# A two-layer trunk on one core: queues reordered, five joints between stages laid out anew, and attention begun inside the last expert tiles

## The chip, the cores and the metric

The kernel runs on one core of a Trainium2 chip. The metric is the device time of one execution in microseconds, as the median of several runs.

## The reference

Input is x, 512 rows of 1024 float32. Two layers follow, each a mixer and an expert block, each behind a root-mean-square norm with a gain, each added to x:

```python
for layer in range(DEPTH):                       # DEPTH = 2
    h = rms_norm(x, norm_mix)
    x = x + (even_mix(h, ...) if layer % 2 == 0 else fox_mix(h, ...))
    h = rms_norm(x, ffn_norm[layer])
    x = x + peer_ffn(h, wq, keys, u, v)
```

`even_mix` projects h to 2576 columns, runs a gated depthwise convolution of width 31 with a layer norm on one half and a chunked gated linear attention on the other, and projects the 1024 results back. `fox_mix` projects h to q, k, v (16 heads of 64) and a forget gate, normalises q and k per head, adds the running sums of the log forget gate to the logits, and takes a causal softmax. `peer_ffn` picks, for each row and each of 8 heads, 16 of 16384 experts by two sets of 128 keys, and adds `gate * gelu(h . u[e]) * v[e]` over these 128 experts.

## The kernel before

**Precision.** Every matmul with a weight is done in three passes: a float32 operand is split into a high part, rounded to float32r by ScalarE, and a low part, the difference, taken by VectorE (or POOL). `split` (line 49) does that, `weight` (54) loads a 128x1024 weight tile into one of four `raw` buffers, and splits it into one of three pairs `whi`, `wlo`; `mm3` (75) issues high x high, high x low and low x high.

**Blocks.** The 512 rows are four blocks of 128. `rms_h` (87) and `rms_body` (95) normalise: per block a square with its sum on ScalarE (104), the factor on VectorE and POOL (105, 106), the scaled rows on VectorE (107) into one of two buffers; then `flip` (109) transposes the block by eight 128x128 matmuls into two PSUM banks (114), from which ScalarE copies the high part (116) and VectorE takes the low part (117) of the transposed `hT`. `hT` has a single buffer pair for all stages.

**Stages.** `build` (1060) runs `mix_even` (228), `peer(0)`, `mix_odd` (542), `peer(1)` (719). The code is unrolled; a tracing framework orders each engine's instructions by a simulated timeline, with program order as priority, and sets the semaphores. `tc.issue_after(i)` ties the instructions traced in it behind instruction `i` on the engine of `i`.

**The mixers** end in `out_proj` (194): two halves of 512 columns, each four weight tiles (`proj_nat`, 145; `nat_parts`, 153) over four accumulators of the six PSUM banks tagged `a`; in the second half the last three weight tiles are swept block by block in the order 1, 2, 3, 0, and each block is added to x. In `mix_odd` the value projection's first half is begun on two leading weight tiles, block by block as the blocks are transposed. Attention's logits, softmax, transposes and values go in 64 units of 128 queries of one head (`unit`, 682), four inside each of 14 q or k projections, the last twelve behind them.

**The expert block** treats block 0 by gathering each row's experts (POOL's indirect loads, lines 861 and 872) and blocks 1 to 3 densely: a first half of 128 tiles (`u_step`, 842: one weight tile, 24 matmuls of 384 columns, a Gelu, a store to `aside`, of which the last 24 stay on chip), during which the gate values are built by small matmuls (`gate4`, 891) and stored to `G`; and a second half of 128 tiles (`prepare`, 962, `v_sweep`, 1022: 18 matmuls of 512 columns into six accumulators). `fetch` (950) loads gates, eight tiles at a time (`gc`), and kept activations, two tiles at a time (`at`). The last three tiles of the second half are swept block by block (1052). `kept` (725) is a copy of blocks 1 to 3 of x in memory, from which x is read back later.

**Queues.** All plain loads and stores are issued by SP, in order; POOL issues the gathers. A load of a weight waits for its `raw` buffer. Line 544 asks for the function table that has logarithm and exponential, tied behind `last_gelu`, which is set by `u_step` (853) and, later, by the gathers' Gelu `g_w` (867).

## Time and profile before

| | us |
|---|---|
| median of 3 runs | 3146.25 (3145.14 to 3149.17) |
| the profiled execution | 3148.14 |
| its span, first to last instruction | 3146.3 |
| mean granted TensorE clock | 0.990 |

The profiled execution is a little longer than its span, by what lies ahead of the first and behind the last instruction. The stages in the span: even mixer to about 271 us, first experts to 1545 (their second half from 1012), attention to 1867, second experts to the end (their second half from 2609). In what follows PE is TensorE's matmuls, PEld its weight loads, DVE VectorE, ACT ScalarE, POOL GpSimd, SP the queue of plain loads. A line of the timeline gives the start, the length, the engine, the source line and what is written from what; in brackets stands the engine's idle time before it and what ended that.

### The profile page before, as it was taken

How to read it: one execution, taken by the hardware profiler on the slowest of the kernel's cores; microseconds unless marked ns; L12 is line 12 of the kernel's file. 1: busy time of each engine (PE TensorE's matmuls, PEld its weight loads, DVE VectorE, ACT ScalarE, POOL GpSimd, SP SyncE). 2: the span in 40 equal slices, each digit the busy share in tenths (PEclk: the TensorE clock that was granted, in tenths of full speed). 3: DMA queues.
4: the chain of work that ended last, by engine and by line, in shares of the span. 5: the costliest groups of instructions: out<-in, count | busy, mean ns of one | idle time of the engine just before them, and what ended most of it. 6: DMA issues, size and time to landing. Idle time of an engine off the chain costs nothing.

```text
span 3146.3 us, 45733 instructions
## 1 busy us (share of the span) xinstructions
PE 3080.9 (98%) x15932; PEld 2696.8 (86%) x15932; DVE 2406.8 (76%) x4936; ACT 1437.2 (46%) x2258; POOL 1155.1 (37%) x800
## 2 busy tenths in 40 slices
PE   8999999999999999999999999999999999999999
PEld 6668999999999888877766679999999998888787
DVE  6765998888885888888535548998888867888786
ACT  4343334666664333333356633336666643333332
POOL 1220122996773332332100000227976752233330
PEclk9999999999999999999999999999999999999999
DMA  4113445999998999999421124448999997999996
GB/s 155 54 34 125 137 140 168 358 351 347 339 323 292 310 350 372 352 350 356 148 81 41 41 77 132 137 144 313 375 340 339 339 322 260 354 367 346 355 349 233
DMA packets 334202, 787.16 MB, mean 250 GB/s; under 512 B 26745, under 2 KB 181770, under 8 KB 327826
## 3 DMA queue, kind: packets, MB, share of 16 engines
q1 hardware_dynamic: 260242, 515.76, 47.0%
q0 software_dynamic: 73728, 268.47, 24.1%
q8 instruction: 125, 2.05, 0.3%
q14 instruction: 107, 0.88, 0.1%
HBM read 687.59 MB, written 96.47 MB: 249 GB/s over the span
## 4 chain that ended last, share of the span: by engine, by line
PE 90%; DVE 3%; DMA 2%; issue 1%; ACT 1%; SPq 1%; POOL 1%; DVEq 0%; ACTq 0%; POOLq 0%
PE acc L1027 33%; PE pu L79 10%; PE pu L78 10%; PE pu L77 10%; PE bank L77 5%; PE bank L79 5%; PE bank L78 5%; PE bank L911 5%; PE po L671 1%; PE pc L284 1%; PE bank L639 1%; PE bank L935 1%; DVE wlo L51 1%; SPq L960 1%; POOL gr L861 1%
## 5 line engine op out<-in xcount | busy, mean ns | idle before, releaser
L50 ACT ACTIVATE whi<-raw 128x1024 fp32r<-128x1024 f32 x604 | 636.9, 1057 | 829.5 <-PE pu L78 471.6
L51 DVE TENSOR_TENSOR wlo<-raw,whi 128x1024 fp32r<-128x1024 f32 x565 | 692.1, 1226 | 183.1 <-ACT whi L50 156.3
L77 PE MATMUL pu<-hhi,whi 128*128 128x384 f32 x2048 | 702.0, 343 | 9.6 <-ACT whi L50 8.7
L79 PE MATMUL pu<-hhi,wlo 128*128 128x384 f32 x2048 | 691.0, 338 | 2.2 <-DVE wlo L51 2.2
L78 PE MATMUL pu<-hlo,whi 128*128 128x384 f32 x2048 | 689.2, 337 | 0.0
L872 POOL DMA_INDIRECT gr<-in_vF_dram,ids x256 | 317.7, 1241 | 717.7 <-DVE x L874 658.7
L1027 PE MATMUL acc<-wlo,wh 128*128 128x512 f32 x1536 | 472.7, 389 | 0.0
L1027 PE MATMUL acc<-whi,wl 128*128 128x512 f32 x1536 | 472.5, 389 | 0.0
L1027 PE MATMUL acc<-whi,wh 128*128 128x512 f32 x1536 | 436.5, 390 | 9.3 <-ACT whi L50 9.3
L861 POOL DMA_INDIRECT gr<-in_uN_dram,ids x256 | 352.5, 1377 | 237.6 <-DVE dots L863 140.7
L50 ACT ACTIVATE wh<-gc 128x384 fp32r<-128x384 f32 x256 | 134.4, 525 | 645.7 <-PE acc L1027 638.0
L77 PEld LDWEIGHTS pu<-hhi,whi 128*128 128x128 f32 x2048 | 388.3, 190 | 12.1 <-ACT whi L50 9.3
L79 PEld LDWEIGHTS pu<-hhi,wlo 128*128 128x128 f32 x2048 | 387.3, 189 | 4.0 <-DVE wlo L51 3.9
L78 PEld LDWEIGHTS pu<-hlo,whi 128*128 128x128 f32 x2048 | 388.1, 190 | 1.9 <-DVE hlo L117 0.6
L1027 PEld LDWEIGHTS acc<-whi,wh 128*128 128x128 f32 x1536 | 287.6, 188 | 72.1 <-ACT whi L50 12.6
L1027 PEld LDWEIGHTS acc<-wlo,wh 128*128 128x128 f32 x1536 | 288.3, 188 | 60.0
L1027 PEld LDWEIGHTS acc<-whi,wl 128*128 128x128 f32 x1536 | 288.3, 188 | 59.8
L901 POOL TENSOR_SCALAR a<-cst,sT 128x128 f32<-128x128 f32 x192 | 330.6, 1722 | 13.2 <-PE bank L911 4.9
L874 DVE SCALAR_TENSOR_TENSOR x<-gr,dots,x 128x1024 f32<-128x1024 f32 x256 | 327.4, 1279 | 0.3
L863 DVE CUSTOM_DVE_ANT_0 gr<-gr,h 128x1024 f32<-128x1024 f32 x256 | 307.9, 1221 | 23.8 <-DMA gr<-in_uN_dram,ids 23.7
L51 DVE TENSOR_TENSOR wl<-gc,wh 128x384 fp32r<-128x384 f32 x256 | 142.7, 558 | 179.4 <-ACT wh L50 170.0
L51 POOL TENSOR_TENSOR wlo<-raw,whi 128x1024 fp32r<-128x1024 f32 x39 | 99.0, 2540 | 398.5 <-ACT whi L50 390.5
(248 smaller groups left out, 4242.3 us busy)
## 6 DMA issues: line engine op xcount, KB each, us to landing
raw<-in_uT_dram SPq DMA_DIRECT2D x256, 512.0 KB
raw<-in_vF_dram SPq DMA_DIRECT2D x256, 512.0 KB
G<-big SPq DMA_DIRECT2D x48, 1024.0 KB
gc<-G SPq DMA_DIRECT2D x32, 1536.0 KB
aside<-xact SPq DMA_DIRECT2D x208, 192.0 KB
at<-aside SPq DMA_DIRECT2D x104, 384.0 KB
raw<-in_w_in_dram SPq DMA_DIRECT2D x32, 512.0 KB
raw<-in_wq_dram SPq DMA_DIRECT2D x32, 512.0 KB
```

Source lines behind the costliest of these rows:

```text
L50: first = self.nc.scalar.activation(hi, raw, AF.Copy)
L51: self.last_lo = (eng or self.nc.vector).tensor_tensor(lo, raw, hi.bitcast(F32), op=ALU.subtract)
L77: mm(out, lh, rh, start=first, stop=False)
L78: mm(out, lh, rl, start=False, stop=False)
L79: return mm(out, ll, rh, start=False, stop=last)
L861: nc.gpsimd.indirect_dma_start(out=r, out_offset=None, in_=uN, in_offset=bass.IndirectOffsetOnAxis(ap=ids[:, s:s + 1], axis=0))
L863: return lambda: nc.vector.tensor_tensor_reduce(r, r, h0, 1.0, 0.0, ALU.mult, ALU.add, accum_out=dots[:, s:s + 1])
L872: nc.gpsimd.indirect_dma_start(out=r, out_offset=None, in_=vF, in_offset=bass.IndirectOffsetOnAxis(ap=ids[:, s:s + 1], axis=0))
L874: return lambda: nc.vector.scalar_tensor_tensor(self.x0, r, dots[:, s:s + 1], self.x0, op0=ALU.mult, op1=ALU.add)
L901: (nc.vector if t else nc.gpsimd).tensor_scalar(a1[:, t], self.iota, e1[:, t:t + 1], gate[:, t:t + 1], op0=ALU.is_equal, op1=ALU.mult)
L911: nc.tensor.matmul(p[:, t], a2[:, t], a1[:, t], start=True, stop=True)
L1027: nc.tensor.matmul(acc[b][c], wt[:, s], vt[:, c], start=(n == 0 and wt is wh and vt is vh), stop=(n == NE1 - 1 and wt is wl))
```

## The change

- **Norms.** `rms_h` and `rms_body` become `norm`, which hands out its steps (`scale`, `flip`, `close`) so that they can be placed one by one. The square writes into the buffer of the scaled rows; there are three or four of these in place of two and a separate square.
- **`chain`** ties each step that it runs behind the last matmul of the step before, on TensorE.
- **Start.** The gain of the first norm is loaded as one row and spread over the partitions by two matmuls with ones and two copies. The blocks of x are asked for next, then four weights (`early`), then the rest of the constants. The step tables are loaded and copied in `peer(0)`, by POOL.
- **`out_proj`** sweeps block by block in a chain, normalises blocks 1 to 3 as each is done, and stores `kept` there. In attention it also runs four units after each weight tile of the first half, and transposes blocks 1 and 2 ahead of block 0's last three sweeps and block 3 ahead of the last of them. After the even mixer the three blocks are transposed behind the sweeps, since `hT` is still in use.
- **`peer`** runs the first expert tile ahead of transposing block 0.
- **Second half of the experts.** `fetch` starts seven tiles (`SETTLE`) after its buffers are opened, its loads are tied behind the last weight's load on SP, and the split of the gates is tied behind the high part of the weight on ScalarE. The split gates have a pool of their own.
- **Into attention.** `odd_begin` runs ahead of the last tiles' sweeps: the function table, tied behind the last Gelu of both kinds, the buffers, and the first two value weights, split ahead into a pool of their own. Sweeps, additions, norms, transposes and the first value sweeps then follow in one chain. The forget gate's projection is moved ahead of the rest of the value projection.
- The convolution's diagonal matrices have three buffers in place of four.

```diff
     def weight(self, src, shape=None, eng=None, after=None, pool=None):
-        raw = self.ws.tile([P, D], F32, tag="raw", name="raw", bufs=4)
-        nc.sync.dma_start(raw, src)
+        raw = self.early.pop(0) if self.early else self.raw(src)
+        if pool:
+            hi, lo = [pool.tile([P, D], F32R, name=x) for x in ("vhi", "vlo")]
...
+    def chain(self):
+        last = []
+        def run(f, *args):
+            if last:
+                with self.tc.issue_after(last.pop().ins):
+                    last.append(f(*args))
+            else:
+                last.append(f(*args))
+            return last[0]
+        return run
...
     def nat_parts(...)
             for kp in order[lead:end]:
-                sweep(load([kp]), range(NB))
+                with self.tc.issue_after(self.last_put.ins) if pool else nullcontext():
+                    ws = load([kp])
+                sweep(ws, range(NB))
...
     def out_proj(self, w, yT, i, order=range(4), hT=None, between=None, middle=None):
...
+            def finish(b):
+                add(1, b, acc[b])
+                if b:
+                    nc.sync.dma_start(self.kept[b - 1], self.xb[b])
+                    scale(b)
+            for b in DB:
+                for f in sweeps:
+                    run(f, b)
+                finish(b)
+            for n, f in enumerate(sweeps):
+                if hT and n == 0:
+                    run(flip, 1, hT)
+                    run(flip, 2, hT)
+                if hT and n == 2:
+                    run(flip, 3, hT)
+                run(f, 0)
+            finish(0)
...
     def mix_even(self):
+        with tc.tile_pool(name="gain", bufs=1, side="right", reuse_waits="tile") as gp:
+            g = gp.tile([1, D], F32, name="g")
+            row = gp.tile([1, P], F32, name="row")
+            nc.vector.memset(row, 1.0)
+            nc.sync.dma_start(g, A["gains"][0:1])
+            for c in range(2):
+                p = self.bank()
+                nc.tensor.matmul(p, row, g[:, c * 512:(c + 1) * 512], start=True, stop=True)
+                nc.scalar.activation(self.grow[:, c * 512:(c + 1) * 512], p, AF.Copy)
+        for b in range(1, NB):
+            nc.sync.dma_start(self.xb[b], A["x"][b * P:(b + 1) * P])
+        self.early = [self.raw(A["w_in0"][i]) for i in (0, 4, 3, 7)]
...
-        with tc.issue_after(self.last_gelu.ins):
+        with tc.issue_after(self.last_gelu.ins), tc.issue_after(self.last_act.ins):
             nc.scalar.preload_act_table_set("natural_log_exp_and_others")
...
     def mix_odd_body(self, hT, sc, rest):
-            vproj(0, rest())
             fh, fl = self.small_weight(sc, A["w_fz"], 16, "wf")
...
+            vproj(0, rest())
...
-            for _ in range(8 + AHEAD + 1):
-                unit()
-            self.out_proj(A["w_out1"], self.rows(oT))
+            self.hT = self.new_hT()
+            self.out_proj(A["w_out1"], self.rows(oT), 3, hT=self.hT, between=lambda: [unit() for _ in range(4)],
+                          middle=lambda: pool.__exit__(None, None, None))
...
     def peer(self, L):
+            if not hT:
+                hT = self.new_hT()
+                for b in DB:
+                    self.run(flip, b, hT)
+            scale(0, h0)
...
     def peer_body(self, L, hT, h0, last, sp, sb):
+        self.run(lambda: u_step(0)[1])
+        nu = 1
+        last()
...
         def fetch(n):
-                nc.sync.dma_start(gcs[m], G[:, :, e * TG:(e + EC) * TG].rearrange("g p n -> p g n"))
+                with tc.issue_after(self.last_raw.ins):
+                    nc.sync.dma_start(gcs[m], G[:, :, e * TG:(e + EC) * TG].rearrange("g p n -> p g n"))
...
-                nc.sync.dma_start(ats[n], aside[e:e + 2].rearrange("e p t -> p e t"))
+                with tc.issue_after(self.last_raw.ins):
+                    nc.sync.dma_start(ats[n], aside[e:e + 2].rearrange("e p t -> p e t"))
...
         def prepare(n):
-            self.split(w, *[t.rearrange("p (g t) -> p g t", t=TG) for t in (wh, wl)])
+            with tc.issue_after(hi.ins):
+                self.split(w, *[t.rearrange("p (g t) -> p g t", t=TG) for t in (wh, wl)])
...
-                vb = vpool.__enter__()
+                wb, vb = wpool.__enter__(), vpool.__enter__()
+                opened = nu
+            if vb and nu == opened + SETTLE:
                 for n in range(-AHEAD, AHEAD):
                     fetch(n)
...
+        if L == 0:
+            hN, (scale, put, _), start = self.odd_begin()
+            with tc.issue_after(self.last_lo.ins):
+                scale(0)
+        run = self.chain()
         for b in range(nd):
-            v_sweep(tail, b)
+            run(v_sweep, tail, b)
             for c in range(2):
                 xa = self.xb[DB[b]][:, c * 512:(c + 1) * 512]
-                nc.vector.tensor_tensor(xa, xa, acc[b][c], op=ALU.add)
+                with tc.issue_after(self.last_xs.ins) if L == 0 else nullcontext():
+                    nc.vector.tensor_tensor(xa, xa, acc[b][c], op=ALU.add)
+            if L == 0:
+                scale(DB[b])
+                if b == 1:
+                    run(put, 0, hN, True)
+        if L == 0:
+            for b in DB:
+                run(put, b, hN, True)
+                run(start, b - 1)
+            run(start, NB - 1)
```

## Rows read from the trace of the kernel before

**Rows 1.** Two parts of the page: busy time of engines, chain that ended last.

```profile
PE 3080.9 (98%) x15932; PEld 2696.8 (86%) x15932; DVE 2406.8 (76%) x4936; ACT 1437.2 (46%) x2258; POOL 1155.1 (37%) x800
...
PE 90%; DVE 3%; DMA 2%; issue 1%; ACT 1%; SPq 1%; POOL 1%; DVEq 0%; ACTq 0%; POOLq 0%
```

**Rows 2.** Windows: start:end, length; busy of PE, PEld, DVE, ACT, POOL; clock; DMA.

```profile
10.00:20.00 10.00, 7.62 (x32) 6.27 (x32) 7.87 (x11) 9.61 (x20) 4.59 (x4) 1.00 0.93 319
20.00:30.00 10.00, 7.38 (x17) 4.89 (x18) 6.24 (x9) 1.80 (x3) 0.54 (x2) 0.66 0.60 193
270.00:290.00 20.00, 15.32 (x76) 13.10 (x75) 11.52 (x15) 8.93 (x14) 1.06 (x2) 0.83 0.32 117
990.00:1010.00 20.00, 15.53 (x77) 14.70 (x76) 6.19 (x9) 8.77 (x11) 2.92 (x3) 0.83 0.88 306
2586.00:2606.00 20.00, 15.31 (x72) 14.48 (x71) 5.96 (x8) 5.73 (x9) 2.63 (x2) 0.83 0.90 320
...
1540.00:1560.00 20.00, 15.79 (x74) 12.82 (x73) 13.59 (x18) 9.09 (x15) 10.57 (x6) 0.91 0.31 105
1580.00:1600.00 20.00, 17.88 (x66) 13.09 (x65) 6.12 (x10) 9.90 (x14) 0.00 (x0) 0.83 0.16 54
1630.00:1640.00 10.00, 8.53 (x32) 5.21 (x31) 6.40 (x17) 7.72 (x14) 0.00 (x0) 0.83 0.16 53
1640.00:1790.00 150.00, 150.00 (x681) 100.96 (x681) 88.94 (x223) 101.81 (x186) 0.00 (x0) 1.00 0.14 43
1790.00:1820.00 30.00, 25.76 (x102) 14.79 (x101) 18.68 (x52) 14.57 (x34) 0.00 (x0) 0.83 0.06 18
1862.00:1892.00 30.00, 24.62 (x107) 20.54 (x106) 15.01 (x22) 11.90 (x19) 3.21 (x4) 0.83 0.30 102
```

**Rows 3.** Timeline of the start: start, length, engine, line; idle before and its releaser.

```profile
9.05 1.28 DVE L107 SCALAR_TENSOR_TENSOR xs<-x,rs,grow 128x1024 f32<-128x1024 f32 x1 [3.21 <-DMA grow<-in_gains_dram]
...
24.61 0.80 PE L78 MATMUL bank<-hlo,whi 128*128 128x512 f32 x1 [1.01 <-DVE hlo L117]
```

**Rows 4.** Timeline, end of the even layer's output projection.

```profile
264.50 1.06 ACT L104 ACTIVATE sq<-x 128x1024 f32<-128x1024 f32 x1 [7.59 <-DVE x L199]
...
266.50 1.29 DVE L107 SCALAR_TENSOR_TENSOR xs<-x,rs,grow 128x1024 f32<-128x1024 f32 x1 [0.66 <-POOL rs L106]
...
271.52 1.91 PE L114 MATMUL bank<-cst,xs 128*128 128x128 f32 x16
...
274.17 2.94 ACT L50 ACTIVATE whi<-raw 128x1024 fp32r<-128x1024 f32 x3
...
277.01 3.02 ACT L116 ACTIVATE hhi<-bank 128x512 fp32r<-128x512 f32 x6
```

**Rows 5.** The chain that ended last, in order of time.

```profile
1020.43 330.54 PE acc L1027 x1458
```

**Rows 6.** Timeline of SP's queue, from first to second half of the experts.

```profile
970.75 6.08 SPq L957 DMA_DIRECT2D gc<-G  x2
976.88 13.76 SPq L960 DMA_DIRECT2D at<-aside  x3
```

**Rows 7.** Waits of TensorE: total us, times, longest.

```profile
PE acc L1027 <- ACT whi L50: 9.3, 8, 1.2
```

**Rows 8.** Timeline of ScalarE in the second half of the experts.

```profile
1351.04 0.52 ACT L50 ACTIVATE wh<-gc 128x384 fp32r<-128x384 f32 x1 [3.56 <-PE acc L1027]
1351.47 1.99 ACT L50 ACTIVATE whi<-raw 128x1024 fp32r<-128x1024 f32 x2
```

**Rows 9.** ScalarE's line groups from 1580 to 1830; timeline before the last units.

```profile
L224 ACT ACT_TABLE_LOAD x16 | 20.5, 1283 | 0.3
L223 ACT ACT_TABLE_LOAD x15 | 19.2, 1283 | 0.3
...
1801.65 0.76 PE L639 MATMUL bank<-ka,qa 66*128 66x128 f32 x2 [3.62 <-issue]
```

**Rows 10.** Timeline, end of attention's output projection.

```profile
1870.57 5.69 PE L114 MATMUL bank<-cst,xs 128*128 128x128 f32 x24 [2.79 <-DVE ss L105]
```

More of the change, by code (lines that the diff above doesn't have):

```diff
@@ L1 @@
+from contextlib import nullcontext
 import concourse.bass as bass
@@ L40 @@
 TAIL = 12
+SETTLE = 7
 NEG = -3.0e38
@@ L85, in load_gain, with norm @@
         self.nc.sync.dma_start(self.grow, self.A["gains"][i:i + 1].to_broadcast([P, D]))
-    def rms_h(self, i, hT, h0=None, order=range(NB), after=None):
-        with self.tc.tile_pool(name=f"rms{i}", bufs=1, reuse_waits="tile") as rp:
-            self.rms_body(rp, i, hT, h0, order, after)
-        if i + 1 < 4:
-            self.load_gain(i + 1)
-    def rms_body(self, rp, i, hT, h0, order, after):
+    def norm(self, i, blocks=3):
         nc = self.nc
+        pool = self.tc.tile_pool(name=f"rms{i}", bufs=1, side="right", reuse_waits="tile")
+        rp = pool.__enter__()
@@ L117, in flip, with close, keep @@
                 nc.vector.tensor_tensor(lo, p, hi.bitcast(F32), op=ALU.subtract)
-        scale(order[0])
-        for n, b in enumerate(order):
-            if n + 1 < NB:
-                scale(order[n + 1])
-            flip(b)
-            if after:
-                after(b)
+            return mm
+        def close():
+            pool.__exit__(None, None, None)
+            if i + 1 < 4:
+                self.load_gain(i + 1)
+        return scale, flip, close
+    def keep(self):
+        self.kept = self.dp.tile([len(DB), P, D], F32, name="kept")
@@ L151, in proj_nat, with nat_parts, load @@
         return rest()
-    def nat_parts(self, srcs, hT, lead=0, order=range(4), done=None, between=None, eng=None):
-        acc = [self.bank() for _ in range(NB)]
-        def load(kps):
-            return [(kp, *self.weight(srcs[kp], (2, 512), eng)) for kp in kps]
+    def nat_parts(self, srcs, hT, lead=0, order=range(4), done=None, between=None, eng=None, pool=None):
+        acc = []
+        def load(kps, pool=None):
+            return [(kp, *self.weight(srcs[kp], (2, 512), None if pool else eng, pool=pool)) for kp in kps]
         def sweep(ws, blocks):
@@ L192, in small_weight, with out_proj @@
         return hi, lo
-    def out_proj(self, w, yT, order=range(4)):
+    def out_proj(self, w, yT, i, order=range(4), hT=None, between=None, middle=None):
         nc = self.nc
@@ L199, in add, with ends @@
             nc.vector.tensor_tensor(xa, xa, acc, op=ALU.add)
-        for b, acc in enumerate(self.proj_nat(w[0], yT, order=order)):
-            add(0, b, acc)
-        self.proj_nat(w[1], yT, order=order, done=lambda b, acc: add(1, b, acc))
+        def ends(sweeps, acc):
+            run = self.chain()
[16 more added lines that the diff above has]
+            finish(0)
+            self.run = run
+        for b, acc in enumerate(self.proj_nat(w[0], yT, order=order, between=between)):
+            add(0, b, acc)
+        if middle:
+            middle()
+        self.keep()
+        self.next_norm = scale, flip, _ = self.norm(i)
+        self.proj_nat(w[1], yT, order=order, done=ends)
     def log_sigmoid(self, sp, z, shape, dst):
```

138 lines of the change are left out of this document (80 added, 58 removed).

## The prediction

> **What bounds the kernel now.** The page comes first: TensorE is busy 98% of the span and is 90% of the chain that ended last [rows 1]. So only time in which TensorE stands still, or runs at its half clock, can be won without removing matmuls, and the change removes none. Next I laid windows over the span, took those where TensorE is not full, and read two prices from each: the idle time (length less busy), and the clock (a granted 0.83 over 20 us means that 6.8 us ran at 1.2 GHz in place of 2.4, worth up to 3.4 us of work). That gives the list of joints [rows 2]: start, 5.0 idle + 3.4 clock between 10 and 30 us, after 10.3 us in which the first scaled rows were not there (9.05 + 1.28 [rows 3]); even layer to first experts (270 to 290), 4.7 + 3.4 = 8.1; first half to second half of the experts, twice, 4.5 + 3.4 = 7.9 and 4.7 + 3.4 = 8.1; first experts to attention, 4.2 + 1.8 = 6.0 and again 2.1 + 3.4 = 5.5 at 1580; the first softmax (1630), 1.5 + 1.7 = 3.2; the last softmax units (1790), 4.2 + 5.1 = 9.3; attention to second experts (1862), 5.4 + 5.1 = 10.5. Outside them the even layer has many small gaps, which the change leaves. The waits, timelines and line groups then say what each joint waits for.
>
> **Part by part.**
>
> **Start.** The first block's scaled rows wait 3.21 us for the gain, a 512 KB broadcast that lands at 9.05; real streaming begins at 24.61 [rows 3]. Now the gain comes as one 4 KB row, spread by two matmuls and two copies, and x and four weights are asked for before the constants. Of the 3.21 us the copies give back about 1.0 (two at 0.50, copies of 512 columns as in [rows 4]: 3.02/6), so some 2 us; 512 KB less stand ahead of x, and the weights no longer wait behind the constants. ScalarE, 9.61 of 10 us busy there [rows 2], sets the rest: two copies added, the two step tables moved to POOL at the first experts, where POOL is idle. Bounds 1 and 7 us; I take 4, because ScalarE stays nearly full. Constants and small tables arrive later: hidden by the first projections.
>
> **Even layer to experts.** Now: 16 transposes in 1.91 us, then three weight splits (2.94) stand ahead of six copies of transposed blocks (3.02, begun at 277.01) on ScalarE, and three more on VectorE [rows 4]. Normalising a block takes 3.3 us from its square (264.50) to its scaled rows (266.50 + 1.29). The third block's scaled rows also waited for one of two buffers; there are three now, and all three blocks are normalised behind block 0's last sweeps. That sweep is 18 matmuls at 0.227 (330.54/1458 [rows 5]) = 4.1 us. Then 24 transposes (2.9 us), copies of 0.50 begun after the first four; expert tile 0 needs only blocks 1 to 3, so it starts about 4 us behind the last sweep rather than 7 or more, and block 0 hides behind it. Block 0's own 3.3 us and its add stand against that tile's 24 matmuls of 384 columns (an estimate: three quarters of 0.227 each, 4.1 us), about even, so a wait of 1 us stays. The transposed buffer is single and still read by the last sweep, so the copies cannot start earlier. Bounds 1 and 6.5, I take 4.
>
> **First to second half of the experts, twice.** SP spends 6.08 us issuing two gate loads and 13.76 us on three loads of kept activations, put ahead of the next weights [rows 6]; the weights land late and TensorE idles. Now one gate load is asked for, seven tiles later and behind a weight, and the rest behind later weights. SP's 20 us there left TensorE idle for some 4; one gate load alone holds SP for at most the 6.08 of two. Bounds 9 and 16 of 16.0; I take 14. Late next: the gate load itself, needed some three tiles on.
>
> **Stream of the second half.** In eight places TensorE waits for the high part of a weight, 9.3 us in all [rows 7], because ScalarE has the gate split (1351.04), which waits for TensorE, ahead of two weight splits (1351.47) [rows 8]. The new order puts each gate split behind its own weight's, so it can no longer overtake. Bounds 3 (the weights then come late from memory: the DMA share there is high) and 9.3; I take 8. Queued behind the gate split is only the next weight, as in the regular tiles now.
>
> **Experts to attention.** The last three tiles' sweeps, 18 matmuls a block, now run in a fixed order; normalisation of block n runs under block n+1, transposes of n and the first two value weights' sweeps alternate behind. After the last sweep stand 8 transposes, 12 matmuls (2.7 us), again 8 and 12: 7.4 us of cover for two adds and the 3.3 us of block 3. The two weights are split by VectorE beforehand, where POOL took longer. The gate projection moves ahead of the rest of the values, whose 48 matmuls (10.9 us) hide the forget-gate chain that idled TensorE at 1587. Of 11.5 us I take 9, bounds 4 and 11.
>
> **Attention's function tables.** ScalarE reloads its table 16 and 15 times between logarithm and exponential, 1.283 us each [rows 9]: the early load of the joint set was placed ahead of the last expert tiles' Gelu and undone by it. The new tie to the last activation repairs that. Most of the 39.7 us is hidden (150 of 150 us TensorE busy from 1640 to 1790 [rows 2]); what shows is the 1630 window: 2 of 3.2, bounds 0 and 3. For the chain before the last units the Trainium skill (ScalarE: Activation LUTs, What ACT_TABLE_LOAD costs) adds a drain, about 2.66 us a switch; by it this chain would shorten by 5.3 us and the sum grow by up to 2.7. By the row the two loads are 2.6, and the sum holds that.
>
> **Last units.** TensorE stands 3.62 us before the last head pair's logits [rows 9] and then runs them at half clock. Twelve units now go, four at a time, between the output projection's first sweeps; 72 matmuls (16 us) stand there to fill the waits. Four of six PSUM banks are held by its sums, so the units have two, which may leave a wait ahead of the last sweep. Of 9.3 I take 7, bounds 3 and 9.3.
>
> **Attention to experts.** TensorE waited 2.79 us for normalisation [rows 10] and later for the low parts. Now blocks 1 and 2 are transposed before block 0's last sweeps and block 3 before the last third, two thirds (2.7 us) plus 16 transposes after its sweep ended: 4.6 us against adds and 3.3. Tile 0 and block 0 as in the even layer. Of 10.5 I take 8.5, bounds 4 and 10.
>
> **Against it.** One scaling buffer fewer for the convolution's diagonal matrices: ScalarE can wait for TensorE on 42 of them; nothing in the profile prices it. Bounds 0 and 4, taken 0.5. The chains fix TensorE's order at each joint, so whatever waits there holds all behind it; that is in the lower bounds.
>
> Sum: 4 + 4 + 14 + 8 + 9 + 2 + 7 + 8.5 - 0.5 = 56 us. The profiled execution took 3148.14 us, 1.8 around a span of 3146.3; the median of the runs is 3146.25, so I subtract from the median: 3090. All lower bounds together give 21, all upper ones 72.
>
> **Rivals.** (a) The joints keep a wait: the chain holds TensorE at the last block's normalisation or copies, the clock falls again, and about half is won. For it: each joint now shows the clock falling after 2 to 4 us of waiting. Against: the covers counted above. 28 us won: 3118. (b) The change does not do what it says in attention: the table load lands ahead of a Gelu again. Then the 1630 window stays, the last units keep some 4 us and the chain at 1587 part of its 5.5: 14 less, 3104. Against: the tie names both last activations. (c) The transposes between sweeps lower the clock: 3.4 us at three joints, 10 less, 3100. The trace speaks against: from 1640 to 1790 transposes stand in every unit and the granted clock is 1.00 [rows 2]. The Trainium skill (TensorE: Matmul & The Clock Gate, PE-mode transpose) says that transposes do not count as busy time for the clock in the same way; by that rule (c) would be likelier, and this trace does not agree. (d) Slower: in the second halves the weights come late at many tiles, since kept activations now stand behind them on SP and the gate split behind the weight's split on ScalarE. Each such wait costs 1.16 (9.3/8 [rows 7]); the 48 us won elsewhere are gone from 41 of 256 tiles on; at every second tile it is 148 us, less those 48: 3246. Against: weights run ahead by four buffers.
>
> **How the numbers follow.** A measurement of this kernel can tell about 0.2% (6 us) from no change. Forecast 0.73, (a) 0.13, (b) 0.06, (c) 0.03, (d) 0.03, and 0.02 that gains and losses cancel. The range goes from 3072, near all upper bounds, to (a)'s 3118; it leaves out (d), the cancelling case and the bad half of (a). Faster 0.95, same 0.02, slower 0.03.
>
> **What would show it.** Right: windows at the same joints with TensorE full and the clock at 1.00; a few table loads in attention at most; no wait of the accumulating matmuls on the weight's high part; SP's gate loads behind weights. Wrong: a new wait of transposes on scaled rows, a half clock at the joints, more idle time in the even layer, or idle time in the second halves.

## The result and the profile after

The changed kernel takes 3111.14 us (median; 3106.74 to 3113.07) against 3145.69 for the kernel before on the same chip: a ratio of 0.989 [0.987, 0.9904]. The forecast was 3090 with a range of 3072 to 3118. So the direction and the range held, and 35 us were won where 56 were summed. The profiled execution took 3110.54, its span is 3108.8 and its mean clock 0.999 (before 3148.14, 3146.3 and 0.990).

The page's busy times and chain, which answer to [rows 1]:

```profile
PE 3064.1 (99%) x15936; PEld 2681.8 (86%) x15936; DVE 2405.2 (77%) x4939; ACT 1386.4 (45%) x2224; POOL 1103.7 (36%) x800
...
PE 83%; DVE 3%; DMA 2%; issue 2%; POOL 1%; ACT 0%; DVEq 0%; POOLq 0%; ACTq 0%
```

TensorE issues four records more (the two gain matmuls, two records each) and is busy 16.8 us less: matmuls at half clock last longer, and few are left. The windows at the joints of [rows 2], in the same columns, moved to where each joint now lies:

```profile
20.00:30.00 10.00, 7.88 (x30) 5.99 (x31) 6.37 (x10) 2.86 (x7) 0.00 (x0) 1.00 0.56 210
30.00:240.00 210.00, 208.70 (x993) 146.06 (x991) 149.51 (x223) 88.26 (x148) 41.44 (x36) 1.00 0.17 55
270.00:290.00 20.00, 14.31 (x71) 13.10 (x71) 10.65 (x15) 8.73 (x14) 1.10 (x2) 0.83 0.41 132
990.00:1010.00 20.00, 20.00 (x117) 20.00 (x116) 10.75 (x17) 7.77 (x13) 3.56 (x3) 1.00 1.06 366
2548.00:2568.00 20.00, 20.00 (x117) 20.00 (x116) 12.52 (x17) 7.39 (x11) 8.30 (x6) 1.00 1.05 385
1580.00:1600.00 20.00, 20.00 (x85) 14.79 (x84) 6.45 (x7) 4.98 (x6) 0.00 (x0) 1.00 0.26 80
1786.00:1836.00 50.00, 46.36 (x202) 32.05 (x201) 21.71 (x44) 13.84 (x28) 0.00 (x0) 1.00 0.17 55
1840.00:1862.00 22.00, 19.83 (x111) 17.02 (x110) 15.03 (x20) 12.16 (x20) 1.65 (x3) 1.00 0.44 152
```

Read the clock column first. Behind the start only 270 to 290, the joint from the even layer to the experts, still holds a half clock (0.83), and there TensorE is less busy than before (14.31 of 20 against 15.32). The 1.00 of 20 to 30 is no measurement up to 25.6: this trace has no entry of the clock ahead of that, and its matmuls of 512 columns follow each other at 0.43 us until 25.3 and at 0.23 from 26.2 on. So the start is still at half clock, until about 25.8; before, it was until 29.9. The 1.00 of 10 to 20 in [rows 2] is no measurement either, since that trace's entries begin at 19.7. Both joints inside the experts are full. Where the last units were, 46.36 of 50 is busy: better, not full.

To add up what every joint won I took, over both traces' matmul records, the interval from each matmul's start to the next one's, less the median interval that its kind has in the kernel before. That counts idle time, half clock and slow pacing alike. In us of the span:

| stretch (us) | lost before | lost after | won | forecast |
|---|---|---|---|---|
| start, 0 to 30, with the time to the first matmul | 22.7 | 21.0 | 1.7 | 4 |
| convolution and rest of the even layer, 30 to 240 | 31.1 | 34.0 | -2.9 | -0.5 |
| even layer to experts, 240 to 300 | 8.1 | 11.7 | **-3.6** | 4 |
| first to second half of the experts, twice | 15.3 | 0.3 | 15.0 | 14 |
| the second halves behind that | 10.5 | -1.4 | 11.9 | 8 |
| experts to attention, 1510 to 1610 | 12.7 | 5.2 | 7.5 | 9 |
| first softmax, 1610 to 1650 | 4.9 | 3.4 | 1.5 | 2 |
| last units, 1790 to 1840 | 10.7 | 6.8 | 3.9 | 7 |
| attention to experts, 1840 to 1900 | 11.5 | 3.3 | 8.2 | 8.5 |
| block 0 in the second experts' first half, 2100 to 2270 | 2.4 | 7.4 | -5.0 | 0 |
| all the rest | 13.4 | 13.7 | -0.3 | 0 |

The sum is 37.9, and the spans differ by 37.5. The row of 2100 to 2270 is code that the change leaves as it is; over all thirteen profiles, of kernels that differ elsewhere, it lies between 2.4 and 7.4, and the 2.4 of the run before is the least of them. The stretches are fixed in the span, so a row's boundary can cut a joint that has moved.

The joint that got worse, from the timeline of the changed kernel (ScalarE's and VectorE's order behind the last sweep):

```profile
273.46 2.78 PE L120 MATMUL bank<-cst,xs 128*128 128x128 f32 x24
274.10 2.07 ACT L122 ACTIVATE hhi<-bank 128x512 fp32r<-128x512 f32 x4 [1.70 <-PE bank L120]
...
276.03 1.08 ACT L109 ACTIVATE h<-x 128x1024 f32<-128x1024 f32 x1
...
277.07 2.02 ACT L53 ACTIVATE whi<-raw 128x1024 fp32r<-128x1024 f32 x2
...
278.18 1.23 DVE L54 TENSOR_TENSOR wlo<-raw,whi 128x1024 fp32r<-128x1024 f32 x1 [0.40 <-ACT whi L53]
278.96 1.10 ACT L122 ACTIVATE hhi<-bank 128x512 fp32r<-128x512 f32 x2
279.32 1.28 DVE L112 SCALAR_TENSOR_TENSOR h<-x,rs,grow 128x1024 f32<-128x1024 f32 x1
279.63 0.45 PE L87 MATMUL pu<-hhi,whi 128*128 128x384 f32 x1 [3.38 <-ACT hhi L122]
280.51 1.22 DVE L54 TENSOR_TENSOR wlo<-raw,whi 128x1024 fp32r<-128x1024 f32 x1
281.65 1.28 DVE L123 TENSOR_TENSOR hlo<-bank,hhi 128x512 fp32r<-128x512 f32 x2
282.39 0.69 PE L88 MATMUL pu<-hlo,whi 128*128 128x384 f32 x1 [2.31 <-DVE hlo L123]
```

ScalarE copies four of the six half blocks, then does block 0's square and two weight splits, and only then the last two. VectorE puts a weight's low part, block 0's scaled rows and another low part ahead of the last two low parts. TensorE, whose first expert matmul needs five of the six (the first half of every block), stands 3.38 and 2.31 us; the half clock comes behind these two waits.

### The profile page after: what moved, and what is told of

It is laid out like the page before. It is cut to its first block, busy times and chain, and to the rows that moved or that the text cites. A ratio compares the mean times of both kernels' runs of the same rounds, so it can differ in the third digit from the quotient of the medians.

```text
span 3108.8 us, 45706 instructions
## 1 busy us (share of the span) xinstructions
PE 3064.1 (99%) x15936; PEld 2681.8 (86%) x15936; DVE 2405.2 (77%) x4939; ACT 1386.4 (45%) x2224; POOL 1103.7 (36%) x800
## 4 chain that ended last, share of the span: by engine, by line
PE 83%; DVE 3%; DMA 2%; issue 2%; POOL 1%; ACT 0%; DVEq 0%; POOLq 0%; ACTq 0%
PE acc L1134 33%; PE pu L88 10%; PE pu L89 10%; PE pu L87 10%; PE bank L1008 5%; PE bank L87 4%; PE bank L89 4%; PE bank L88 4%; DMA gr<-in_uN_dram,ids 2%; PE po L763 1%; PE bank L731 1%; PE bank L1036 1%; DVE wlo L54 1%; DVE gr L960 1%; PE bank L750 1%
## 5 line engine op out<-in xcount | busy, mean ns | idle before, releaser
L969 POOL DMA_INDIRECT gr<-in_vF_dram,ids x256 | 278.0, 1086 | 719.9 <-DVE x L971 695.5
L1134 PE MATMUL acc<-wlo,wh 128*128 128x512 f32 x1536 | 439.1, 389 | 0.0
L1134 PE MATMUL acc<-whi,wl 128*128 128x512 f32 x1536 | 437.4, 389 | 0.0
L995 DVE TENSOR_TENSOR a<-cst,sT 128x512 f32<-128x512 f32 x192 | 132.8, 692 | 125.8 <-PE bank L1008 117.6
L87 PE MATMUL bank<-hhi,whi 128*128 128x512 f32 x512 | 210.5, 412 | 3.1 <-ACT hhi L122 3.1
```

The lines of the kernel that those rows point to most:

```text
L87: mm(out, lh, rh, start=first, stop=False)
L969: nc.gpsimd.indirect_dma_start(out=r, out_offset=None, in_=vF, in_offset=bass.IndirectOffsetOnAxis(ap=ids[:, s:s + 1], axis=0))
L1134: mm = nc.tensor.matmul(acc[b][c], wt[:, s], vt[:, c], start=(n == 0 and wt is wh and vt is vh), stop=(n == NE1 - 1 and wt is wl))
```

## The experiments

Where no range is given, an experiment has one time. The kernel before, run beside them, took 3144.55 (median of 7; beside the joint's order, the early table load, the queue and three diagonal buffers), 3147.48 (one time; beside the squares ahead of the copies, the gate split, the table tie and the units) and 3145.46 (median of 9; the rest). Times of the kernel before differ by up to 8 us within one such set, so a single time shows little by itself, and the windows are read first.

**The order at the joint.** Block 0's square is tied behind the last copies, its scaled rows behind the last low parts, and the first tile's Gelu is moved behind block 0's copies:

```diff
-                nc.vector.tensor_tensor(lo, p, hi.bitcast(F32), op=ALU.subtract)
+                self.last_hlo = nc.vector.tensor_tensor(lo, p, hi.bitcast(F32), op=ALU.subtract)
...
-            scale(0, h0)
+            with tc.issue_after(self.last_put.ins), tc.issue_after(self.last_hlo.ins):
+                scale(0, h0)
...
-        self.run(lambda: u_step(0)[1])
+        late = []
+        self.run(lambda: u_step(0, late=late)[1])
         nu = 1
         last()
+        with tc.issue_after(self.last_put.ins):
+            late[0]()
```

> The changed kernel with two ties at the joint from a mixer to the experts: block 0's square stands on ScalarE, and its scaled rows on VectorE, behind the last copies of the transposed blocks 1 to 3; the Gelu of expert tile 0 stands behind the copies of block 0. Theory (order on the two small engines): the chain orders TensorE alone, and block 0's norm and two weight splits got ahead of block 3's copies (from 276.0 to 279.0 us), so TensorE idled 3.38 + 2.31 us ahead of tile 0 and ran 6.8 us at half clock, and 1.67 behind it. Then the window from 270 to 297 loses 6 to 9 us less, the second such joint about 1 less, and the kernel takes 3101 to 3105 against 3111. Rival (the single transposed buffer, released by the last sweep, sets the start of the copies): the idle time only moves to other waits in the same window, and the time stays within 2 us of 3111.

Measured: 3101.69 (3100.39 to 3101.96), ratio to the kernel before 0.9863 [0.9846, 0.9879]; 9.4 us less than the changed kernel. Its window and timeline at the joint:

```profile
270.00:290.00 20.00, 18.14 (x96) 16.07 (x95) 13.19 (x18) 11.87 (x18) 1.10 (x2) 0.91 0.52 165
```

```profile
274.22 3.05 ACT L122 ACTIVATE hhi<-bank 128x512 fp32r<-128x512 f32 x6 [1.70 <-PE bank L120]
...
275.36 3.67 DVE L123 TENSOR_TENSOR hlo<-bank,hhi 128x512 fp32r<-128x512 f32 x6
276.83 0.44 PE L87 MATMUL pu<-hhi,whi 128*128 128x384 f32 x1 [0.46 <-ACT hhi L122]
...
278.48 0.56 PE L88 MATMUL pu<-hlo,whi 128*128 128x384 f32 x1 [1.21 <-DVE hlo L123]
```

Six copies run in a row, the waits shrink from 3.38 and 2.31 to 0.46 and 1.21, and TensorE is busy 18.14 of 20. By the table's measure the joint won 6.4 (11.7 to 5.3, and 8.1 in the kernel before); 2.5 of the other 3.0 lie in the stretch that varies from run to run. That the order on ScalarE and VectorE cost this joint its gain is shown. The clock is still 0.91: 3.4 us at half clock follow the second wait.

**The table load alone.** In the kernel before, the early load is tied behind the tiles' last Gelu too:

```diff
-        with tc.issue_after(self.last_gelu.ins):
+        with tc.issue_after(self.last_gelu.ins), tc.issue_after(self.last_act.ins):
...
-            self.last_gelu = nc.scalar.activation(a, p, AF.Gelu)
+            self.last_act = nc.scalar.activation(a, p, AF.Gelu)
```

> The kernel before with one part of the change: the request for the joint logarithm and exponential table is tied behind the last expert Gelu as well as the gathers' Gelu. Theory one (the prediction's split): the tables show only at the first softmax and a little ahead of the last units, 2 to 5 us: about 3141. Theory two: most of what the change won inside attention comes from the tables, since each of the waits at 1587, 1633 and 1798 us stands at the end of a chain with two or three loads of 1.283 us in it, and each is followed by a half clock; then these three go and the time is 3146 - (5.5 + 3 + 6) = about 3131.

Measured: 3137.16. The windows that answer to 1580 to 1600 and 1790 to 1820 of [rows 2]:

```profile
1580.00:1600.00 20.00, 19.96 (x86) 14.10 (x84) 10.03 (x14) 8.08 (x12) 0.00 (x0) 1.00 0.25 80
1785.00:1815.00 30.00, 28.97 (x133) 17.64 (x132) 17.05 (x48) 13.42 (x33) 0.00 (x0) 1.00 0.06 19
```

Both were at a clock of 0.83 before, with 17.88 of 20 and 25.76 of 30 busy. This one tie wins, by the table's measure, 5.1 us in 1570 to 1610 and 8.2 in 1790 to 1840. The total, 7 us below the kernel before, is less than these 13: the stretch of 2100 to 2270 lost 4 more in this run. So the tie is worth far more than the 2 us of my sum, where it stands alone, but none of it lies at the first softmax, for which the sum had it: there TensorE waits 1.43 us for VectorE in all thirteen profiles, with the loads or without, and 1610 to 1650 loses 4.9 us with the tie as before. What differs there from run to run is whether a half clock follows that wait (before, and with the tie alone, it does; in the changed kernel it does not).

**The table load not repaired.** The counterpart, in the changed kernel:

```diff
-        with tc.issue_after(self.last_gelu.ins), tc.issue_after(self.last_act.ins):
+        with tc.issue_after(self.last_gelu.ins):
```

> The changed kernel with the table request tied as before, behind the gathers' Gelu only. Theory two of the tables: the loads come back, some 30, and attention loses 3 to 8 us more, less than the 13 that the tie wins alone on the kernel before, since the forget-gate chain and the last units now have cover: about 3116. Rival (the prediction's split, where the moved work is what counts): at most 2 us more.

Measured: 3109.27, no slower than the 3111.14 with the tie. ScalarE's groups from 1540 to 1880, as [rows 9]:

```profile
L280 ACT ACT_TABLE_LOAD x16 | 20.5, 1283 | 0.3
L279 ACT ACT_TABLE_LOAD x15 | 19.2, 1283 | 0.3
```

These 31 loads are back, with two single ones beside them 42 us of ScalarE, and cost nothing: from 1510 to 1840 the measure of the table finds 22.4 us lost, with the tie 22.1. The moved gate projection and the moved units put matmuls over the same two gaps, so where they stand the tie has nothing left to win. My sum counted both. The load not repaired with the units left in front was not tried.

**The last units back ahead of the output projection**, with the tie kept:

```diff
-            self.out_proj(A["w_out1"], self.rows(oT), 3, hT=self.hT, between=lambda: [unit() for _ in range(4)],
+            for _ in range(8 + AHEAD + 1):
+                unit()
+            self.out_proj(A["w_out1"], self.rows(oT), 3, hT=self.hT,
```

> The changed kernel with the last twelve softmax units put back ahead of the output projection. Theory: inside the projection they have two PSUM banks in place of six, and their waits of 0.4 to 0.8 us there are waits for banks; with the tables mended the place that they were moved from cost only 2.5 us (the tables kernel), so going back wins 2 to 4 us between 1780 and 1840: about 3108. Rival: the move is what closed the last units' gap, and going back loses 3 us or more there.

Measured: 3104.32, 6.8 us less than the changed kernel's median. The window of this kernel, then two of the changed kernel's matmuls that wait:

```profile
1780.00:1830.00 50.00, 49.25 (x221) 35.84 (x222) 21.33 (x46) 13.24 (x27) 0.00 (x0) 1.00 0.16 51
```

```profile
1800.77 1.12 PE L731 MATMUL bank<-ka,qa 66*128 66x512 f32 x2 [0.69 <-ACT PT L753]
...
1809.98 0.91 PE L731 MATMUL bank<-ka,qa 66*128 66x384 f32 x2 [0.65 <-DVE PT L755]
```

With the units moved, a unit's logits wait for the bank from which the unit before is being copied (the prediction's "the units have two"); with them in front, 49.25 of 50 are busy in place of 46.36. Behind a repaired table the move of the units costs 5.4 us by the table's measure (6.8 to 1.4).

**SP's queue alone.** The kernel before, with the loads of gates and kept activations tied behind the last weight and begun seven tiles later:

```diff
-        nc.sync.dma_start(raw, src)
+        self.last_raw = nc.sync.dma_start(raw, src)
...
+                with tc.issue_after(self.last_raw.ins):
+                    nc.sync.dma_start(gcs[m], G[:, :, e * TG:(e + EC) * TG].rearrange("g p n -> p g n"))
...
-                nc.sync.dma_start(ats[n], aside[e:e + 2].rearrange("e p t -> p e t"))
+                with tc.issue_after(self.last_raw.ins):
+                    nc.sync.dma_start(ats[n], aside[e:e + 2].rearrange("e p t -> p e t"))
...
                 vb = vpool.__enter__()
+                opened = nu
+            if vb and nu == opened + 7:
```

> The kernel before with another part alone: gate and activation loads tied behind the last weight's load on SP, and the first of them issued seven tiles later. Theory: the two waits of 4.2 and 4.5 us for a weight at the turn from first to second half go, with their half clock, and with them the eight waits of 1.16 us in the second half stay, since those come from ScalarE's order: about 3131. Rival: the eight waits came from late weights, and go as well: about 3121.

Measured: 3135.36. Its windows at both joints, and its longest waits of TensorE by total:

```profile
990.00:1010.00 20.00, 20.00 (x115) 19.70 (x114) 10.92 (x20) 11.73 (x17) 3.26 (x2) 1.00 0.97 329
2586.00:2606.00 20.00, 20.00 (x110) 18.99 (x109) 10.09 (x14) 8.73 (x13) 0.09 (x1) 1.00 0.68 210
```

```profile
PE acc L1031 <- ACT whi L50: 9.3, 8, 1.2
```

Both joints are full, by this part alone, and the eight waits for the weight's high part are untouched. The first of SP's gate loads in the changed kernel's timeline (two took 6.08 us together in [rows 6]; the second now takes 0.38 as well, 20.6 us later; in this run the two take 0.38 each, too) shows why:

```profile
976.12 0.38 SPq L1059 DMA_DIRECT2D gc<-G  x1
```

**The gate split not tied**, in the changed kernel:

```diff
-            with tc.issue_after(hi.ins):
+            if True:
                 self.split(w, *[t.rearrange("p (g t) -> p g t", t=TG) for t in (wh, wl)])
```

> The changed kernel without the tie of the gate split behind the weight's high part. Theory: ScalarE's order alone made the eight waits, and they come back with it: 8 times 1.16 us, with what the streams lose around them 10 to 12 us, so about 3122. Rival: the loads' new order on SP had removed them already (the queue kernel alone, on the older code, kept all eight, which speaks against): the time stays within 3 us of 3111.

Measured: 3118.42. The timeline of the first of the eight, which answers to [rows 8]:

```profile
1348.85 0.61 PE L1134 MATMUL acc<-whi,wl 128*128 128x512 f32 x2
...
1349.10 0.52 ACT L53 ACTIVATE wh<-gc 128x384 fp32r<-128x384 f32 x1 [3.56 <-PE acc L1134]
...
1350.62 1.67 PE L1134 MATMUL acc<-whi,wh 128*128 128x512 f32 x6 [1.16 <-ACT whi L53]
```

All eight waits of 1.16 are back. It also shows the size that I had too small: two matmuls begin at 1348.85, and at 0.227 each the next could start at 1349.30; it starts at 1350.62. That is 1.32, not 1.16, since the row counts idle time from a modelled end; eight of them are 10.6. By the table's measure the second halves lose 12 more than in the changed kernel. The total rose by only 7.3, since two stretches lost less: 2.2 us in the one that varies, and 2.8 at the joint to attention (5.2 to 2.4). There the order on VectorE came out otherwise without the tie, and the three waits of transposes on scaled rows (2.8 us together in the changed kernel) became one of 0.86, for a low part.

**The start: squares ahead of the copies.** In the changed kernel, the two copies that spread the gain are tied behind the first block's square:

```diff
-        def scale(b, dst=None):
+        def scale(b, dst=None, mid=None):
...
             self.last_sq = nc.scalar.activation(xs[b], self.xb[b], AF.Square, accum_out=ss)
+            if mid:
+                mid()
...
-                nc.scalar.activation(self.grow[:, c * 512:(c + 1) * 512], p, AF.Copy)
+                with tc.issue_after(self.last_sq.ins):
+                    nc.scalar.activation(self.grow[:, c * 512:(c + 1) * 512], p, AF.Copy)
```

> The changed kernel with the two copies of the spread gain tied behind block 0's square on ScalarE, in place of ahead of all squares. Theory: the start won 2.6 us of the 4 forecast because the two spreading matmuls take 3.75 us at the start and the squares stand behind their copies: block 0's square begins at 9.20 though x was there at 4.5. Then the first scaled rows come 1 to 2 us earlier and streaming starts up to 2 us earlier. Rival: the start is set by the sum of ScalarE's and VectorE's work (with POOL's split slowing VectorE) up to the last block's copies, and streaming starts within 0.7 us of where it did.

Measured: 3109.64. The changed kernel's timeline, then this one's:

```profile
4.92 3.75 PE L296 MATMUL bank<-g,row 1*128 1x512 f32 x4 [4.92 <-DMA g<-in_gains_dram]
...
8.70 0.60 ACT L297 ACTIVATE grow<-bank 128x512 f32<-128x512 f32 x1 [1.11 <-PE bank L296]
...
9.20 1.05 ACT L109 ACTIVATE xs<-x 128x1024 f32<-128x1024 f32 x1
...
11.22 1.28 DVE L112 SCALAR_TENSOR_TENSOR xs<-x,rs,grow 128x1024 f32<-128x1024 f32 x1 [0.69 <-POOL rs L111]
...
14.48 2.36 POOL L54 TENSOR_TENSOR wlo<-raw,whi 128x1024 fp32r<-128x1024 f32 x1 [0.76 <-ACT whi L53]
14.50 3.42 DVE L112 SCALAR_TENSOR_TENSOR xs<-x,rs,grow 128x1024 f32<-128x1024 f32 x1
...
18.06 1.94 PE L120 MATMUL bank<-cst,xs 128*128 128x128 f32 x8 [1.52 <-DVE xs L112]
...
25.82 0.50 PE L88 MATMUL bank<-hlo,whi 128*128 128x512 f32 x1
```

```profile
4.48 1.06 ACT L109 ACTIVATE xs<-x 128x1024 f32<-128x1024 f32 x1 [2.47 <-DMA x<-in_x_dram]
...
9.79 0.58 ACT L304 ACTIVATE grow<-bank 128x512 f32<-128x512 f32 x1
...
10.48 5.79 DVE L114 SCALAR_TENSOR_TENSOR xs<-x,rs,grow 128x1024 f32<-128x1024 f32 x3 [0.41 <-ACT grow L304]
...
20.00 1.94 PE L122 MATMUL bank<-cst,xs 128*128 128x128 f32 x8 [2.52 <-DVE xs L114]
...
24.24 0.80 PE L88 MATMUL bank<-hlo,whi 128*128 128x512 f32 x1
```

```profile
20.00:30.00 10.00, 9.99 (x28) 7.11 (x29) 4.79 (x8) 2.07 (x5) 0.00 (x0) 0.57 0.43 138
```

The square begins at 4.48 in place of 9.20, but the first scaled rows come only 0.74 earlier: they wait for the second copy of the gain, at 9.79, which stands behind two more squares on ScalarE although the gain's matmuls end at 8.67. The last block's transposes, at 20.00 for 22.12, still wait for scaled rows. Streaming, taken as the first matmul with the low part of a block, starts 1.58 us earlier (24.24 for 25.82), but at half clock until 28.6, where the changed kernel's matmuls are at full pace from about 25.8: TensorE is busy 9.99 of 10 in the window and gets 28 matmuls through it, the changed kernel 30 in 7.88. The 200th projection matmul starts at 73.1 (changed kernel 72.6, before 73.9, counted in the traces). Nothing is won.

**The start: POOL off the first weight.** As before, and the first weight's low part on VectorE:

```diff
-                pv = self.proj_T(wi[i], hT, nc.gpsimd if i == 0 else None)
+                pv = self.proj_T(wi[i], hT)
```

> The start kernel (gain copies behind block 0's square) with the first weight's low part taken by VectorE in place of POOL. Theory: VectorE sets the start; its scaled rows take 3.4 us in place of 1.28 while POOL's split of 2.4 to 2.8 us runs beside them, so without that split the three rows of 5.79 us take 3.9 and streaming starts about 1 us earlier, although VectorE has 1.22 us more to do. Rival: the start is set by ScalarE and by the arrival of x; the streaming starts no earlier than in the start kernel.

Measured: 3109.51. The same three blocks' scaled rows:

```profile
10.85 3.68 DVE L114 SCALAR_TENSOR_TENSOR xs<-x,rs,grow 128x1024 f32<-128x1024 f32 x3 [0.40 <-ACT grow L304]
```

3.68 in place of 5.79: beside POOL's split VectorE lost 2.1 us. But the low part that POOL no longer makes is VectorE's now, the first matmul with the low part of a transposed block starts at 23.64 for 24.24, at half clock until 28.0, and the total stays.

**The diagonal buffers**, once by themselves in the kernel before (four to three), once undone in the changed kernel (three to four, with the even mixer's pool closed ahead of the second half of its output projection to make room):

```diff
-                        dg = sb.tile([P, P], F32, name="dg", bufs=4)
+                        dg = sb.tile([P, P], F32, name="dg", bufs=3)
```

```diff
-        with tc.tile_pool(name="m0", bufs=1) as sp, tc.tile_pool(name="m0b", bufs=2) as sb:
+        with tc.tile_pool(name="m0", bufs=1) as sp:
+            pool = tc.tile_pool(name="m0b", bufs=2)
+            sb = pool.__enter__()
...
-                        dg = sb.tile([P, P], F32, name="dg", bufs=3)
+                        dg = sb.tile([P, P], F32, name="dg", bufs=4)
...
-            self.out_proj(A["w_out0"], self.rows(yb), 1, (2, 3, 0, 1))
+            self.out_proj(A["w_out0"], self.rows(yb), 1, (2, 3, 0, 1),
+                          middle=lambda: pool.__exit__(None, None, None))
```

> The kernel before with three buffers in place of four for the convolution's diagonal matrices, nothing else. Theory: this is the 3 us that the changed kernel lost between 30 and 240 us; here TensorE loses 2 to 4 us more in that stretch. Rival: those 3 us come from the moved start, and this kernel loses nothing there (within 1 us).

> The changed kernel with four buffers for the diagonal matrices and nothing else but the room for them. Theory: the kernel before loses 2.5 us between 30 and 240 us with three; here that comes back, the stretch loses 31 to 32 where it lost 34.0, and the time is about 3108. Rival: the loss hangs on the order around the start of each kernel, and nothing comes back.

Measured: 3150.58 with three buffers in the kernel before, 3104.19 with four in the changed one, 7.0 less than the changed kernel. By the table's measure 2.5 and 2.8 us of these differences lie between 30 and 240. The window of 30 to 240 of the kernel before, of it with three, and of the changed kernel with four:

```profile
30.00:240.00 210.00, 208.69 (x1005) 147.51 (x1004) 150.72 (x225) 89.77 (x150) 44.35 (x36) 1.00 0.17 55
```

```profile
30.00:240.00 210.00, 208.84 (x993) 146.17 (x992) 149.08 (x223) 88.33 (x148) 42.02 (x36) 1.00 0.18 55
```

```profile
30.00:240.00 210.00, 208.59 (x1004) 147.50 (x1003) 152.23 (x227) 90.83 (x151) 43.58 (x36) 1.00 0.17 56
```

Busy time says nothing here (208.6 to 208.8 each time): the count of matmuls does. Three buffers get 993 through this window, four get 1004 or 1005; twelve at 0.227 are 2.7 us. So the loss is slower pacing that the page calls busy. The matmuls that read the diagonal matrices do not carry it: by the table's measure they lose 10.2 us with three buffers and 12.7 with four, in either kernel. Others lose more instead (the linear attention's q by k products 3.1 for 2.0, the projections' passes most of the rest). Why fewer buffers slow those was not settled.

**The three repairs together.** The joint's order, the units in front and four diagonal buffers, each with the edit shown above.

> The changed kernel with three edits together: the joint's ties on ScalarE and VectorE, the last twelve softmax units ahead of the output projection again, and four buffers for the convolution's diagonal matrices (room is made by closing the even mixer's work buffers ahead of the output projection's second half). The effects lie in different stretches, so they should add: 9 (joint) + 6 (units) + 2.5 (buffers) = 17.5 under 3111, about 3093.5; if the stretches trade time among them, 3096 to 3100.

Measured: **3093.7** (3090.61 to 3095.4), ratio to the kernel before 0.983 [0.9817, 0.9844], 17 us below the changed kernel, as the expectation added it up; this is the best version. The single times, 9.4, 6.8 and 7.0 below the changed kernel, would add up to 23. By the table's measure the joint won 8.4 (11.7 to 3.3), the last units 4.2 (6.8 to 2.6) and the convolution 2.8. Two of its windows:

```profile
270.00:290.00 20.00, 18.14 (x104) 15.87 (x103) 13.14 (x17) 11.21 (x17) 0.55 (x1) 1.00 0.50 160
1786.00:1836.00 50.00, 49.72 (x224) 38.99 (x224) 21.37 (x27) 13.83 (x20) 1.65 (x3) 1.00 0.27 92
```

The waits at the joint are those of the joint's order alone (0.46 and 1.22 us), and TensorE is busy the same 18.14 of 20; but no half clock follows them here, and 104 matmuls get through in place of 96. Why the clock fell in one run and not in the other is open, so 2 us of the joint's gain are not shown to be an edit's.

## Why the prediction was right or wrong

**Right.** Only idle time and half clock could be won, and were. Of the parts, the two joints inside the experts (14 forecast, 15.0 won) and attention to experts (8.5, 8.2) came as summed, and the late gate load does what it was said to do [rows 6]. The tie removes the table loads, as it was to. Rival (d), slower second halves, did not come: no wait of the accumulating matmuls on a weight is left.

**Where the prediction was wrong: even layer to experts.** The failed step is "copies of 0.50 begun after the first four; expert tile 0 needs only blocks 1 to 3, so it starts about 4 us behind the last sweep ... and block 0 hides behind it". The first expert matmul with a high part began 6.2 us behind the first transpose and streaming 8.9 (282.39 - 273.46). I counted the copies as if ScalarE and VectorE did nothing else, though [rows 4] shows weight splits ahead of them, and let block 0 hide behind the tile although nothing kept its square behind the copies. The change fixed TensorE's order only; the order on the other two engines was left to the framework. The experiment on the joint's order gives back 6.4 us there: the first expert matmul then begins 3.2 us behind the first transpose and streaming 4.9, near the 4 that I summed. Block 0 does then fit: its transposes follow the tile at 284.16 without a wait.

**Double counting.** The table tie, the gate projection and the units were added as if independent. Near 1590 the tie alone wins 5.1 and the moves alone 5.3 of the same 6.4. At the last units the tie alone wins 8.2 of 10.7, the move 3.9 with or without the tie; so with the tie in place the move costs. The 2 us that I booked for the first softmax are a wrong term: the tables do not cause the wait there, and the 1.5 that were won are a half clock that did not come this time, luck by what the runs show. The clause "the units have two, which may leave a wait ahead of the last sweep" was right in kind, but the wait comes between units.

**Sizes.** The stream of the second half won 11.9 for 8: 1.32 us a wait, not the row's 1.16, and the range's upper end should have said so. Experts to attention won 7.5 for 9: three waits of transposes on scaled rows stay, 2.8 us together. No run was made for them, but without the gate split's tie they were gone, so they hang on the order that the framework finds, and not on the work alone. The diagonal buffers cost 2.5 to 2.8 for 0.5, inside their bounds of 0 to 4, but not as waits at the diagonal matrices.

**The start** won 1.7 for 4. The failed step is "of the 3.21 us the copies give back about 1.0": the gain's matmuls, left out of the sum, took 3.75 us, and the copies stand ahead of the squares, so the first scaled rows come at 11.22 (before 9.05 [rows 3]). What is won is that the half clock ends at about 25.8 in place of 29.9, which is eight matmuls fewer at 0.43 us in place of 0.23, or 1.6 us; streaming itself starts 1.2 us later than before (25.82 for 24.61 [rows 3]). The two experiments on the start, of which the second holds the first, bring streaming forward by 1.6 and 2.2 us and gain nothing, since TensorE then runs at half clock until 28.6 and 28.0. So the start is bounded by when the clock rises, and not by the rows alone; the sum had no term for that.

**Rival (c)**, transposes lowering the clock at three joints, did not come. In the version with three repairs the same 24 transposes stand between the last sweep and the experts, and the window's clock is 1.00; so it is at the joint from attention to the experts (1840 to 1862), and no half clock stands in the changed kernel's trace between 288 and 3107 us. In the changed kernel it fell in the second of two waits, 5.7 us together. A part of the transposes in it is not excluded: with the joint's order alone 24 transposes and waits of only 1.7 us stood ahead of 3.4 us at half clock. The Trainium skill (TensorE: Matmul & The Clock Gate, PE-mode transpose) says that such transposes do not count as busy in the same way; no half clock of this case followed transposes without a wait, and the transposes with the same waits went with either clock.

**Rival (a)**, half the gain kept back by waits, is what came at one joint of five; the other four kept most of what was summed. The total, 3111.14, nevertheless lies nearer to its 3118 than to 3090, and 5 us of the difference to the forecast, a quarter, lie in the varying stretch by the profiled executions; with single parts changed the kernel before lost 2.4 to 6.5 there, so that part is luck.

## What to carry to other kernels

When a change fixes one engine's order at a joint, write down the order of every engine that feeds it, and tie what is not needed yet (prefetched weights, the next block's norm) behind what is: an in-order engine that is 45% busy can still hold the critical copy back by 3 us. Before adding two gains, ask whether each alone would close the same gap, and test each by taking it away from the finished kernel as well as by adding it to the old one. Where a stretch reads fully busy, count its matmuls.

## What the runs showed of the hardware

- **VectorE beside POOL.** One block's scaled rows (two operands from on-chip memory) took 1.28 us alone and 3.42 beside POOL's split of 14.48 to 16.84, ending 1.08 after it: nearly its whole own length. The Trainium skill (SBUF — State Buffer, Who interferes with whom) says that a VectorE instruction with two inputs in on-chip memory contends with a GpSimd instruction that reads it, and calls the port pair that the two share an exclusive lock; these rows agree, and the run with the split taken off POOL got its 2.1 us back.
- **The start can run at half clock with a window that reads 1.00**: the changed kernel's trace has no entry of the clock ahead of 25.6 us, and eight transposes took 1.94 us at 18.06, while 24 took 2.78 at 273.46 (0.24 against 0.12 each). In the run with the joint's order, whose start is the same code, entries begin at 15.8: full clock until 19.2, where eight transposes take 1.06 at 17.96, then half until 26.1, where eight take 1.94 at 22.03.
- **The same waits, two clocks.** The first softmax's wait of 1.43 us came with a half clock in five of the thirteen profiles, and the waits of 0.46 and 1.2 us at the joint in one of two. A gain of some 2 us at such a place can be chance.
- **Function tables.** 33 loads, 42 us of ScalarE, cost no measurable time where matmuls covered them; taking them out of the kernel before won some 13 us by the table's measure, in two stretches.
- **A stretch of unchanged code** (2100 to 2270, where small gate matmuls wait for POOL) lost 2.4 to 7.4 us in different runs; the cause is open.
